# Turning the rows of a second RMSNorm by VectorE block transposes and a round trip through DRAM, instead of by TensorE

## The chip, the cores and the metric

One core of a Trainium2 chip runs the whole kernel in one launch. The metric is the device time of the execution in microseconds (us); lower is better. Engines are named as in the profile: PE is TensorE, PEld its weight loads, DVE is VectorE, ACT is ScalarE, POOL is GpSimd, SP is SyncE, which here only issues DMAs. L970 is line 970 of the kernel before.

## The reference

A single decoder layer with 1024 tokens (and 16 meta tokens), width 1024, feed-forward width 4096, all in fp32. Cut to what matters here:

```python
mix = jnp.concatenate([attn, rec], axis=-1) @ w_out[l]
h = h + rmsnorm(mix, g_post_mix[l])
u = rmsnorm(h, g_pre_ffn[l])                       # the second norm
f = jnp.square(jax.nn.relu(u @ w_ff1[l])) @ w_ff2[l]
h = h + rmsnorm(f, g_post_ffn[l])
```

`u` is computed with a token on each partition, since the norm sums over the width. The product with `w_ff1` contracts over the width, so `u` is needed with the width on the partitions: it has to be transposed.

## The kernel before

Matrix products are done in three matmuls each, on operands split into a high and a low part (`split`, L94: ACT casts the high part, DVE subtracts it from the source for the low part; `mm3`, L123).

The output projection works on eight tiles of 128 tokens (the loop at L1112). For tile t, `out_mm` puts 48 matmuls of 512 columns into two PSUM banks (for tiles 0 to 3 all but 12 of these are done ahead). `out_norm` (L937) then does the following, for each tile:

- SP loads the tile's rows of x into a slot of the ring "d" (four slots) (L939).
- ACT squares both halves out of PSUM and sums them (L944); POOL raises the mean to the power -0.5 (L176).
- DVE scales both halves by that and the gain (L950) and adds the row of x (L953); SP stores the result to the output (L954).
- ACT squares the sum (L956), POOL makes its root (L170, L176), and DVE multiplies by it (L958) into the slot of "d".

`u2_tiles` (L961) turns such a tile: eight 128x128 transposes on PE (L970) into two PSUM banks, each evicted with the gain of the width on its partitions, the first four chunks by ACT (L981), the other four by DVE, two chunks at once (L975). The eight calls stand by hand between the output matmuls of tiles 4 to 7 and behind them (L1115, L1118, L1147). The results, `u2f[half][i]`, are eight tiles of [128, 2, 512] in the ring "c": two chunks of the width by the 512 tokens of one half.

What follows is a feed-forward layer with seven products in place of eight (Strassen's scheme). `operand` (L998) splits the first half's tiles: `b11` after tile 5, `b21` after tile 6. `p1` and `p2` (L1102, L1107) are the first products, of the first half alone. `t_sums` (L1138) forms sums of both halves (L996) and splits them, first for tiles 4 to 6 (three quarters of the columns), later for tile 7. `prep_a` (L1019) loads a pair of weight blocks into the rings "raw" and "d" or "a", sums them on DVE and splits them; `early` (L1045) loads weights ahead. `t_rest` (L1160) makes the later sums.

The order on each engine is set by the program's order as priority, with a planner's estimate of when things are ready; a few orders are written by hand (`behind`). DMAs on SP's queue are issued in order, so a DMA that waits holds up those behind it. Slots of a ring are handed out in turn: whoever takes a slot waits until its last reader is done. "raw" has two slots, "d" four, "ws" five.

Of the kernel before, what the change touches and what calls it, by code (L numbers as in the profile page):

```python
# [9 lines left out]
F32 = mybir.dt.float32  # L10
# [6 lines left out]
P = 128  # L17
D = 1024
# [19 lines left out]
def hybrid_layer(  # L38
# [311 lines left out]
    def transposed(b, xn, after=None):  # L350
        t0, n = ALL[b]
        for kc in range(KC):
            flip[0] += 1
            pt = bank(("pt", "o", "s")[flip[0] % 3])
            o = 0
            for s, m in xn:
                ins = nc.tensor.transpose(
                    pt[:, o : o + m], s[:m, kc * P : (kc + 1) * P], ident[:m, :m]
                )
                if after:  # L360
                    behind(after, ins.ins)
                o += m
            if b == 0:
                load(1, P, ins.ins.name)
            uh, ul = u[kc]
            if b == 0 and kc in (0, 1):
                key_casts.pop(0)()
            high = split_scaled(
                uh[:, t0 : t0 + n], ul[:, t0 : t0 + n], pt[:, :n],
                g_mix_col[:, kc : kc + 1],  # L370
            )
            if b == 0:
                chained(0, high[0])
                chained(1, high[1])

    def fetch(cols, tag="raw", pieces=1):
        raw = slot(tag, [P, KC, P])
# [539 lines left out]
    t4_dram = dpool.tile([P, 2, 4, 512], F32, name="t4_dram")  # L917

    u2f = [[None] * 4 for _ in range(2)]

    def out_mm(t, po, kcs):
        half, o = t // 4, (t % 4) * P
# [8 lines left out]
                )  # L931

    def out_banks(t):
        tag = ("pt", "o", "acc", "s", "pt", "acc", "s", "pt")[t]
        return [bank(tag), bank(tag)]

    def out_norm(t, po):  # L937
        xr = slot("d", [P, D])
        nc.sync.dma_start(xr, x[t * P : (t + 1) * P, :])  # L939
        h = slot("raw", [P, D])  # L940
        ssq = [small.tile([P, 1], F32, name=f"sq{n}", tag=f"sq{n}") for n in range(2)]
        for n in range(2):
            c = slice(512 * n, 512 * n + 512)
            nc.scalar.activation(  # L944
                h[:, c], po[n], AF.Square, scale=RMS_SC, accum_out=ssq[n]
            )
        rs = rstd_of(ssq)
        for n in range(2):
            c = slice(512 * n, 512 * n + 512)
            nc.vector.scalar_tensor_tensor(  # L950
                h[:, c], po[n], rs, gmix_b[:, c], op0=ALU.mult, op1=ALU.mult
            )
        nc.vector.tensor_tensor(h, h, xr, op=ALU.add)  # L953
        nc.sync.dma_start(out[t * P : (t + 1) * P, :], h)  # L954
        ssq2 = small.tile([P, 1], F32, name="ssq", tag="ssq")
        nc.scalar.activation(xr, h, AF.Square, scale=RMS_SC, accum_out=ssq2)  # L956
        rs2 = rstd_of([ssq2])
        nc.vector.tensor_scalar(xr, h, rs2, None, op0=ALU.mult)  # L958
        return xr

    def u2_tiles(t, xn):  # L961
        half = t // 4
        if u2f[half][0] is None:
            u2f[half] = [slot("c", [P, 2, 512]) for _ in range(4)]
        o = (t % 4) * P
        for k4 in range(0, KC, 4):
            pt = bank("o", (P, 4, P))
            for i in range(4):
                kc = k4 + i
                nc.tensor.transpose(pt[:, i, :], xn[:, kc * P : (kc + 1) * P], ident)  # L970
            for i in range(0, 4, 2):
                kc = k4 + i
                dst = u2f[half][kc // 2]
                if k4:
                    nc.vector.tensor_tensor(  # L975
                        dst[:, :, o : o + P], pt[:, i : i + 2, :],
                        g_ffn_col[:, kc : kc + 2].to_broadcast([P, 2, P]), op=ALU.mult,
                    )
                    continue
                for n in range(2):  # L980
                    nc.scalar.activation(  # L981
                        dst[:, n, o : o + P], pt[:, i + n, :], AF.Copy,
                        scale=g_ffn_col[:, kc + n : kc + n + 1],
                    )

# [9 lines left out]
    def combine(dst, x0, x1, op):  # L995
        return nc.vector.tensor_tensor(dst, x0, x1, op=op).ins  # L996
# [115 lines left out]
    for t in range(8):  # L1112
        po = pos[t] if t < 4 else out_banks(t)
        out_mm(t, po, range(6 if t < 4 else 0, KC))
        for t_ in {4: (0,), 5: (2,), 6: (4,), 7: (5,)}.get(t, ()):  # L1115
            u2_tiles(t_, xns[t_])
        xns[t] = out_norm(t, po)
        for t_ in {4: (1,), 5: (3,), 7: (6,)}.get(t, ()):  # L1118
            u2_tiles(t_, xns[t_])
        if t == 4:  # L1120
            a11_early.update(early(0, 0, pair("a", ESH)))
        if t == 5:
            b11 = operand(u2f[0][0:2])
# [7 lines left out]
        p1(p, a11_early[p])  # L1131
    for p in range(2):
        p2(p, a12_early[p])
    t3 = [slot("a", [P, 2, 512]) for _ in range(2)]
    t2 = [slot("a", [P, 2, 512]) for _ in range(2)]
    ot2 = [pair("b", [P, 2, 512]) for _ in range(2)]

    def t_sums(c):  # L1138
        for i in range(2):
            combine(t3[i][:, :, c], u2f[1][2 + i][:, :, c], u2f[1][i][:, :, c], ALU.subtract)  # L1140
            combine(t2[i][:, :, c], t3[i][:, :, c], u2f[0][i][:, :, c], ALU.add)
            hi, lo = ot2[i]
            split(hi[:, :, c], lo[:, :, c], t2[i][:, :, c])

    t_sums(slice(0, 3 * P))
    wa[0] = prep_a(0)
    u2_tiles(7, xns[7])  # L1147
    t_sums(slice(3 * P, 4 * P))
    urgent = mark[0]
    for p in range(2, 4):  # L1150
        p1(p, a11_early[p])
# [1 line left out]
    p2(2, a12_early[2])  # L1153
    ot3 = [pair("b", [P, 2, 512]) for _ in range(2)]
    for i in range(2):
        behind(urgent, split(*ot3[i], t3[i]))
    wa[1] = prep_a(1, urgent)


    def t_rest(k):  # L1160
        i = k % 2
        if k < 2:
            behind(mark[0], combine(u2f[1][i], u2f[1][i], u2f[0][i], ALU.subtract))
        elif k < 4:
            behind(mark[0], combine(t2[i], u2f[0][2 + i], t2[i], ALU.subtract))
        else:
            hl = pair("a", [P, 2, 512])
            late = mark[0]
            behind(late, split(*hl, t2[i]))
# [339 lines left out]
```

## Time and profile before

| | |
|---|---|
| median of 3 runs | 955.24 us (955.24 to 955.97) |
| span of the profiled execution, first to last instruction | 955.3 us |
| mean granted TensorE clock | 0.998 |
| the part that the change touches | about 261 to 352 us of the span |
| DMA traffic over the span | 130.21 MB, mean 136 GB/s |

The profile is one execution, taken by the hardware profiler. The span agrees with the runs to 0.1 us. Busy times of PE overlap, since matmuls are pipelined: a matmul of 512 columns is shown as 0.39 us long, but the next starts 0.23 us later. So lengths of PE's work are read from start to start. A timeline row is: start, length, engine, line, operation, out<-in with shapes, and in brackets how long the engine had been idle and what ended that. A row of groups is: line, engine, operation, shapes, count | busy us, mean ns | idle time before.

### The profile page before, as it was taken

How to read it: one execution, taken by the hardware profiler on the slowest of the kernel's cores; microseconds unless marked ns; L12 is line 12 of the kernel's file. 1: busy time of each engine (PE TensorE's matmuls, PEld its weight loads, DVE VectorE, ACT ScalarE, POOL GpSimd, SP SyncE). 2: the span in 40 equal slices, each digit the busy share in tenths (PEclk: the TensorE clock that was granted, in tenths of full speed). 3: DMA queues.
4: the chain of work that ended last, by engine and by line, in shares of the span. 5: the costliest groups of instructions: out<-in, count | busy, mean ns of one | idle time of the engine just before them, and what ended most of it. 6: DMA issues, size and time to landing. Idle time of an engine off the chain costs nothing.

```text
span 955.3 us, 12432 instructions
## 1 busy us (share of the span) xinstructions
PE 943.8 (99%) x4728; PEld 789.7 (83%) x4728; DVE 655.7 (69%) x845; ACT 505.9 (53%) x854; POOL 129.1 (14%) x189
## 2 busy tenths in 40 slices
PE   9999999999999999999999999999999999999996
PEld 8999999877888878888888888888887788888885
DVE  6567987788856787665644465476667576779893
ACT  7537766568645554444655575654433343446441
POOL 4102563520021100010000000001121100001201
PEclk9999999999999999999999999999999999999999
DMA  8221010204226368674422364334777765647934
GB/s 271 56 67 23 24 45 24 67 23 131 83 109 185 133 220 264 198 253 144 155 89 88 111 203 127 104 113 114 175 180 186 185 199 177 192 139 196 246 65 89
DMA packets 88199, 130.21 MB, mean 136 GB/s; under 512 B 13702, under 2 KB 52630, under 8 KB 88140
## 3 DMA queue, kind: packets, MB, share of 16 engines
q1 hardware_dynamic: 78972, 104.44, 34.0%
q0 software_dynamic: 8880, 24.19, 12.2%
q8 instruction: 37, 0.61, 0.3%
q10 hardware_dynamic: 288, 0.79, 0.2%
q14 instruction: 22, 0.18, 0.1%
HBM read 109.93 MB, written 18.87 MB: 135 GB/s over the span
## 4 chain that ended last, share of the span: by engine, by line
PE 88%; DVE 5%; ACT 3%; DMA 2%; POOL 1%; issue 1%; SPq 0%; DVEq 0%; ACTq 0%; POOLq 0%
PE ps_acc L130 10%; PE ps_acc L131 10%; PE ps_acc L125 10%; PE ps_s L131 6%; PE ps_s L130 6%; PE ps_s L125 6%; PE ps_pt L130 6%; PE ps_pt L131 6%; PE ps_pt L125 6%; PE ps_o L130 5%; PE ps_o L131 5%; PE ps_o L125 5%; ACT c L82 1%; PE ps_o L691 1%; PE ps_acc L282 1%
## 5 line engine op out<-in xcount | busy, mean ns | idle before, releaser
L99 DVE TENSOR_TENSOR ws<-raw,ws 128x1024 fp32r<-128x1024 f32 (+1 forms) x69 | 82.6, 1197 | 76.1 <-ACT ws L96 24.3
L96 ACT CAST ws<-raw 128x1024 fp32r<-128x1024 f32 (+1 forms) x68 | 69.7, 1026 | 87.9 <-PE ps_o L130 23.9
L96 ACT CAST ws<-e 128x1024 fp32r<-128x1024 f32 x41 | 43.0, 1049 | 82.8 <-PE ps_o L130 35.3
L125 PE MATMUL ps_acc<-a,ws 128*128 128x256 f32 (+2 forms) x256 | 85.8, 335 | 0.0
L130 PE MATMUL ps_acc<-a,ws 128*128 128x256 f32 (+2 forms) x256 | 85.5, 334 | 0.0
L131 PE MATMUL ps_acc<-a,ws 128*128 128x256 f32 (+2 forms) x256 | 85.0, 333 | 0.0
L99 DVE TENSOR_TENSOR b<-b,b 128x1024 fp32r<-128x1024 f32 (+2 forms) x50 | 58.9, 1177 | 24.8 <-PE ps_o L130 19.1
L96 ACT CAST b<-b 128x1024 fp32r<-128x1024 f32 (+2 forms) x49 | 49.9, 1019 | 46.4 <-DVE b L996 41.0
L99 DVE TENSOR_TENSOR ws<-e,ws 128x1024 fp32r<-128x1024 f32 x41 | 50.1, 1223 | 32.4 <-ACT ws L96 18.9
L680 POOL TENSOR_SCALAR_AFFINE_SELECT c<-c 128x512 fp32r<-128x512 f32 x64 | 53.6, 858 | 67.6 <-ACT c L96 59.3
L125 PEld LDWEIGHTS ps_acc<-a,ws 128*128 128x128 f32 x256 | 48.3, 189 | 4.7 <-issue 0.2
L131 PEld LDWEIGHTS ps_acc<-a,ws 128*128 128x128 f32 x256 | 48.3, 189 | 4.5
L130 PEld LDWEIGHTS ps_acc<-a,ws 128*128 128x128 f32 x256 | 48.2, 188 | 4.4 <-issue 0.4
L125 PE MATMUL ps_acc<-ws,b 128*128 128x512 f32 (+1 forms) x120 | 46.3, 387 | 1.1 <-ACT ws L96 1.1
L130 PE MATMUL ps_acc<-ws,b 128*128 128x512 f32 (+1 forms) x120 | 46.3, 386 | 0.5 <-DVE ws L99 0.4
L131 PE MATMUL ps_acc<-ws,b 128*128 128x512 f32 (+1 forms) x120 | 46.1, 385 | 0.0
L125 PE MATMUL ps_pt<-ws,b 128*128 128x512 f32 x112 | 44.4, 396 | 0.0
L130 PE MATMUL ps_pt<-ws,b 128*128 128x512 f32 x112 | 44.1, 394 | 0.0
L131 PE MATMUL ps_pt<-ws,b 128*128 128x512 f32 x112 | 44.0, 393 | 0.0
L125 PE MATMUL ps_s<-ws,b 128*128 128x512 f32 x110 | 43.4, 395 | 0.0
L131 PE MATMUL ps_s<-ws,b 128*128 128x512 f32 x110 | 43.3, 394 | 0.0
L130 PE MATMUL ps_s<-ws,b 128*128 128x512 f32 x110 | 43.3, 393 | 0.0
(416 smaller groups left out, 2662.0 us busy)
## 6 DMA issues: line engine op xcount, KB each, us to landing
raw<-in_w_ff_dram SPq DMA_DIRECT2D x61, 512.0 KB, 4.1
e<-in_w_ff_dram SPq DMA_DIRECT2D x45, 512.0 KB, 4.0
a<-in_w_ff_dram SPq DMA_DIRECT2D x12, 512.0 KB, 6.6
s_dram<-a POOLq DMA_DIRECT2D x12, 512.0 KB, 3.7
c<-in_x_dram SPq DMA_DIRECT2D x8, 512.0 KB, 4.0
raw<-in_w_in_dram SPq DMA_DIRECT2D x8, 512.0 KB, 3.7
d<-in_x_dram SPq DMA_DIRECT2D x8, 512.0 KB, 3.3
out_dram<-raw SPq DMA_DIRECT2D x8, 512.0 KB
```

What stands on the lines that cost most here:

```text
L82: ins = nc.scalar.activation(*args, **kwargs).ins
L96: nc.scalar.copy(hi, src)
L99: low = nc.vector.tensor_tensor(lo, src, f32(hi), op=ALU.subtract).ins
L125: ins = nc.tensor.matmul(dst, lh, rh, start=start, stop=False, skip_group_check=True).ins
L130: nc.tensor.matmul(dst, lh, rl, start=False, stop=False, skip_group_check=True)
L131: last_mm[0] = nc.tensor.matmul(dst, ll, rh, start=False, stop=stop, skip_group_check=True).ins.name
L282: last_mm[0] = nc.tensor.matmul(acc[:, :n], w[k // 2][:, kc, :], u[kc][k % 2][:, t0 : t0 + n], start=k == 0 and kc == 0, stop=k == last an ...
L680: nc.gpsimd.affine_select(out=p_[:, :, s], in_=f32(p_[:, :, 0]), pattern=[[0, 4], [g, P]], compare_op=op, fill=0.0, base=0, channel_multip ...
L691: nc.tensor.matmul(po[:, oc : oc + n], v, p_[:, pc : pc + n], start=first and k == 0, stop=last and k == 1, skip_group_check=True,)
```

## The change

Tiles 0 to 6 (`LAST_BY_DMA = 6`) are no longer turned by PE. Instead `out_norm` multiplies the tile by the root and by the gain at once, with the gain broadcast over all partitions (`gpre_b`, a new slot of "ws", loaded once by an ACT DMA). Then `blocks` lets DVE transpose blocks of 32x32 into a second slot of "d" (`y`): it reads each run of 32 elements with a step of four, so that partition p of the result collects what the write then puts in order. One DMA writes the 512 KB to a DRAM scratch with rows of 4 KB. `u2_read`, called one tile later, fetches it by four DMAs of 128 KB, each with runs of 64 floats (256 bytes), straight into the four tiles `u2f[half][i]`. All five transfers are on SP's queue. Tile 7 still goes over PE.

For this the layout of `u2f`, `t2` and `t3` changes from [128, 2, 512] to [128, 16, 2, 32], groups of 32 tokens outermost; `split` writes back into [128, 2, 512] through a rearranged view (`rows`). The evictions of tile 7 are single chunks on both engines. Tile 7's PSUM banks are those of the ring "o" instead of "pt".

```diff
+    def blocks(y, src, dram):
+        nc.vector.transpose(
+            y.rearrange("p (b k t) -> p b k t", b=4, k=KC),
+            src.rearrange("p (k d b) -> p b k d", k=KC, b=4),
+        )
+        nc.sync.dma_start(dram.rearrange("a (d b) r -> (a d) (b r)", b=4), y)
+
+    def unblock(dst, dram, i, n):
+        w = 2 * P // n
+        nc.sync.dma_start(
+            dst.rearrange("p a k t -> p a (k t)"),
+            dram[:, :, w * i : w * i + w].rearrange("a p r -> p a r"),
+        )
...
+    LAST_BY_DMA = 6
+    u2_dram = dpool.tile([LAST_BY_DMA + 1, 4, P, 2 * P], F32, name="u2_dram")
+    gpre_b = slot("ws", [P, D])
+    nc.scalar.dma_start(gpre_b, g_pre_ffn[0].partition_broadcast(P))
...
-        tag = ("pt", "o", "acc", "s", "pt", "acc", "s", "pt")[t]
+        tag = ("pt", "o", "acc", "s", "pt", "acc", "s", "o")[t]
...
-        nc.vector.tensor_scalar(xr, h, rs2, None, op0=ALU.mult)
-        return xr
+        if t > LAST_BY_DMA:
+            nc.vector.tensor_scalar(xr, h, rs2, None, op0=ALU.mult)
+            return xr
+        nc.vector.scalar_tensor_tensor(
+            xr, h, rs2, gpre_b, op0=ALU.mult, op1=ALU.mult
+        )
+        blocks(slot("d", [P, D]), xr, u2_dram[t])
...
+    def u2_read(t):
+        g = slice(4 * (t % 4), 4 * (t % 4) + 4)
+        for i, dst in enumerate(u2_half(t // 4)):
+            unblock(dst[:, g], u2_dram[t], i, 4)
...
+                    d_ = dst[:, g, n]
+                    s_ = pt[:, i + n, :].rearrange("p (a t) -> p a t", a=4)
+                    col = g_ffn_col[:, kc + n : kc + n + 1]
+                    if k4:
+                        nc.vector.tensor_scalar(d_, s_, col, None, op0=ALU.mult)
+                    else:
+                        nc.scalar.activation(d_, s_, AF.Copy, scale=col)
...
+    def rows(tile_, c=slice(0, 16)):
+        return tile_.rearrange("p k (g t) -> p g k t", t=32)[:, c]
...
-            split(hi, lo, t_)
+            split(rows(hi), rows(lo), t_)
...
-        for t_ in {4: (0,), 5: (2,), 6: (4,), 7: (5,)}.get(t, ()):
-            u2_tiles(t_, xns[t_])
         xns[t] = out_norm(t, po)
-        for t_ in {4: (1,), 5: (3,), 7: (6,)}.get(t, ()):
-            u2_tiles(t_, xns[t_])
+        if t:
+            u2_read(t - 1)
```

More of the change, by code (lines that the diff above doesn't have):

```diff
@@ L972, in u2_tiles @@
                 kc = k4 + i
[L973 to L979, printed above, removed]
[L980 to L984 removed]
+                dst = u2_half(t // 4)[kc // 2]
+                for n in range(2):
+                    d_ = dst[:, g, n]
[5 more added lines that the diff above has]
+                        nc.scalar.activation(d_, s_, AF.Copy, scale=col)
     w1v = w_ff1.rearrange("(b k p) c -> b p k c", b=2, p=P)
@@ L1133, in hybrid_layer @@
         p2(p, a12_early[p])
-    t3 = [slot("a", [P, 2, 512]) for _ in range(2)]
-    t2 = [slot("a", [P, 2, 512]) for _ in range(2)]
+    t3 = [slot("a", [P, 16, 2, 32]) for _ in range(2)]
+    t2 = [slot("a", [P, 16, 2, 32]) for _ in range(2)]
     ot2 = [pair("b", [P, 2, 512]) for _ in range(2)]
@@ L1139, in t_sums @@
         for i in range(2):
-            combine(t3[i][:, :, c], u2f[1][2 + i][:, :, c], u2f[1][i][:, :, c], ALU.subtract)
-            combine(t2[i][:, :, c], t3[i][:, :, c], u2f[0][i][:, :, c], ALU.add)
+            combine(t3[i][:, c], u2f[1][2 + i][:, c], u2f[1][i][:, c], ALU.subtract)
+            combine(t2[i][:, c], t3[i][:, c], u2f[0][i][:, c], ALU.add)
             hi, lo = ot2[i]
-            split(hi[:, :, c], lo[:, :, c], t2[i][:, :, c])
-    t_sums(slice(0, 3 * P))
+            split(rows(hi, c), rows(lo, c), t2[i][:, c])
+    t_sums(slice(0, 12))
     wa[0] = prep_a(0)
     u2_tiles(7, xns[7])
-    t_sums(slice(3 * P, 4 * P))
+    t_sums(slice(12, 16))
     urgent = mark[0]
@@ L1155, in hybrid_layer @@
     for i in range(2):
-        behind(urgent, split(*ot3[i], t3[i]))
+        behind(urgent, split(*map(rows, ot3[i]), t3[i]))
     wa[1] = prep_a(1, urgent)
@@ L1168, in t_rest @@
             late = mark[0]
-            behind(late, split(*hl, t2[i]))
+            behind(late, split(*map(rows, hl), t2[i]))
             for n in range(2):
```

9 lines of the change are left out of this document (5 added, 4 removed).

## The prediction

> **What bounds the kernel now.** I read the page first, then the chain that ended last, then the windows and the timelines of TensorE (PE) and VectorE (DVE) around the second norm.
>
> ```profile
> span 955.3 us, 12432 instructions
> PE 943.8 (99%) x4728; PEld 789.7 (83%) x4728; DVE 655.7 (69%) x845; ACT 505.9 (53%) x854; POOL 129.1 (14%) x189
> PE 88%; DVE 5%; ACT 3%; DMA 2%; POOL 1%; issue 1%; SPq 0%; DVEq 0%; ACTq 0%; POOLq 0%
> ```
>
> PE is busy for 99% of the span, and 88% of the chain is PE. So time taken out of PE's queue is worth its full length, unless another engine is close behind it. The windows show where that is so:
>
> ```profile
> 261.00:282.00 21.00, 21.00 (x93) 17.02 (x92) 11.13 (x17) 9.32 (x24) 5.40 (x10) 1.00 0.26 101
> 320.00:335.00 15.00, 15.00 (x78) 12.50 (x77) 12.56 (x21) 8.85 (x23) 2.40 (x4) 1.00 0.55 176
> 335.00:352.00 17.00, 16.94 (x74) 13.34 (x73) 16.20 (x27) 11.83 (x18) 0.56 (x2) 1.00 0.58 189
> ```
>
> After window and length come PE, PEld, DVE, ACT and POOL busy, then the granted clock, the DMA share and GB/s. Until 320 us DVE has slack; from 335 to 352 it works 16.20 of 17.00 us. The chain runs through exactly that stretch:
>
> ```profile
> 319.70 0.87 PE ps_o L970 x8
> 323.39 0.59 ACT d L1105
> 324.03 1.16 ACT d L956 x2
> 325.58 0.99 POOL rs L176
> 326.59 0.26 DVE d L958
> ...
> 350.49 0.61 DVE e L99
> 351.15 0.50 PE ps_acc L131
> ```
>
> The chain leaves PE at 323.4, passes through the last norm (L956, L176, L958 of tile 7), then stays on DVE (with a weight load in between) and gives back to PE at 351.15. There PE is only just not waiting. So whatever PE gains ahead of that point counts only as far as DVE's work moves forward too.
>
> **What the change takes from PE.** It removes seven of the eight groups of eight transposes at L970.
>
> ```profile
> 281.73 0.39 PE L131 MATMUL ps_pt<-a,b 128*128 128x512 f32 x1
> 281.96 1.03 PE L970 MATMUL ps_o<-ident,d 128*128 128x128 f32 x8
> 282.75 0.48 PE L125 MATMUL ps_acc<-ws,b 128*128 128x512 f32 x1
> 283.07 0.40 PE L130 MATMUL ps_acc<-ws,b 128*128 128x512 f32 x1
> ```
>
> Matmuls start every 0.23 us. Without the group the two after it would start at 281.96 and 282.19; the second starts at 283.07, so a group costs 0.88 us of PE. Seven cost **6.2 us**, the most that the change can bring by PE. Five groups stand ahead of the end of tile 7's output matmuls (319.5 us), so that end moves forward by 5 x 0.88 = **4.4 us**. The other two lie between it and 351.
>
> **What it takes from and gives to DVE.** Rows of the groups by form, and one tile's turn in DVE's timeline:
>
> ```profile
> L958 DVE TENSOR_SCALAR d<-raw,rs 128x1024 f32<-128x1024 f32 x8 | 6.0, 754 | 12.8 <-POOL rs L176 12.8
> L975 DVE TENSOR_TENSOR c<-ps_o,gcol 128x256 f32<-128x256 f32 x16 | 6.0, 415 | 0.0
> L953 DVE TENSOR_TENSOR raw<-raw,d 128x1024 f32<-128x1024 f32 x8 | 9.8, 1224 | 0.2
> L1343 DVE SCALAR_TENSOR_TENSOR a<-b,rs,ws 128x1024 f32<-128x1024 f32 x4 | 5.1, 1279 | 0.0
> ...
> L851 DVE TENSOR_TENSOR_SCAN c<-b,c 128x1040 f32<-128x1040 f32 x2 | 4.6, 2314 | 0.0
> ...
> 264.39 1.41 DVE L950 SCALAR_TENSOR_TENSOR raw<-ps_pt,rs,e 128x512 f32<-128x512 f32 x2 [0.75 <-POOL rs L176]
> 275.74 1.41 DVE L950 SCALAR_TENSOR_TENSOR raw<-ps_acc,rs,e 128x512 f32<-128x512 f32 x2
> 280.58 0.75 DVE L958 TENSOR_SCALAR d<-raw,rs 128x1024 f32<-128x1024 f32 x1 [2.10 <-POOL rs L176]
> 281.40 1.41 DVE L950 SCALAR_TENSOR_TENSOR raw<-ps_s,rs,e 128x512 f32<-128x512 f32 x2
> 321.28 1.41 DVE L950 SCALAR_TENSOR_TENSOR raw<-ps_pt,rs,e 128x512 f32<-128x512 f32 x2
> ```
>
> Per tile two evictions of 415 ns go, 0.75 us as a pair in the timeline. The scaling by the row's root grows from a tensor_scalar to a scalar_tensor_tensor with the broadcast gain: 1.28 - 0.75 = +0.53 us. New is the block transpose of 128x1024. The trace has no transpose on DVE and no read with a step of four elements. It can't cost less than the cheapest pass over 128x1024, 0.75 us; the dearest pass over as many elements is the scan, 2.31 us. I take **1.22 us**, the row of the plain two-operand pass at L953, since a transpose too has to move each element once, and keep 0.75 and 2.31 for the range.
>
> In the stretch where eight tiles follow each other, DVE runs one tile's turn after the other: L950, L953, a wait for ACT and POOL, L958, next tile. From 275.74 to 281.40 that is 5.66 us. With the change a turn is 5.66 + 0.53 + 1.22 = 7.41 us if the transpose stands ahead of the next tile's L950. Tile 7's L950 then comes no sooner than 264.39 + 7 x 7.41 = 316.3 us. PE would let it come at 321.28 - 4.4 = 316.9. The two nearly meet: DVE's turns become almost the bound, with 0.6 us to spare. The weight and operand splits that also lie here must fit into the waits of some 2.1 us per turn (the row at 280.58). In sum that fits, but not each one; I charge **0.6 us**.
>
> Within the chain's stretch after L958 of tile 7, tile 6's pair of evictions (0.75) goes; tile 7's second four chunks are now evicted by four instructions instead of two, for which no row exists: I charge 0.4 for them (two more starts of short instructions; bounds 0 and 0.8). Net -0.35. The sums and splits at L996 and L99 see other strides of whole 32-element runs; I cost them at nothing, since the rows at L996 that already read halves of a row run at the speed of the others:
>
> ```profile
> L996 DVE TENSOR_TENSOR raw<-raw 128x512 f32<-128x512 f32 x16 | 10.9, 688 | 0.3
> L99 DVE TENSOR_TENSOR b<-b,b 128x512 fp32r<-128x512 f32 x4 | 2.7, 679 | 0.0
> ```
>
> ACT loses 28 evictions and gains one DMA issue for the gain; ACT was ahead of nothing here. The changed bank for tile 7 (tile 1's) is long free.
>
> **The transfers.** Each tile now writes 512 KB and reads it back in four parts with runs of 256 bytes.
>
> ```profile
> 270.38 0.60 ACT L944 ACTIVATE raw<-ps_acc 128x512 f32<-128x512 f32 x1 [2.13 <-DMA out_dram<-raw]
> ...
> 267.08 11.68 SPq L954 DMA_DIRECT2D out_dram<-raw  x3
> ...
> L208 SPq DMA_DIRECT2D raw<-in_w_in_dram x13: 368/368/817, 23.0 to 170.8; - x13
> ...
> DMA to landing us min/median/max: 3.0/3.6/3.7
> ...
> s_dram<-a POOLq DMA_DIRECT2D x12, 512.0 KB, 3.7
> ...
> a<-in_w_ff_dram SPq DMA_DIRECT2D x12, 512.0 KB, 6.6
> ```
>
> A write of 512 KB lands after 3.3 (issued 267.08, its waiter starts at 270.38) to 3.7 us, loads in pieces of 64 columns (L208, the same 256-byte runs) after 3.0 to 3.7, and an issue holds SP 0.37 us. For tiles 0 to 5 there is room: their operands are split after 305. Tile 6 decides. Its turn ends at 316.3 at the earliest (where tile 7's L950 starts); the write lands by 320.4; its reads stand behind tile 7's store, which waits for L953 of tile 7 (316.9 + 1.41 + 1.14 = 319.5). So four issues run from 320.4 to 321.9 and the last lands at about 325.2. What reads tile 6 first, the sums of three tiles, starts now at 328.52 and should move to 328.52 - 4.4 - 0.75 = 323.4:
>
> ```profile
> 328.52 0.95 DVE L996 TENSOR_TENSOR a<-c,c 128x768 f32<-128x768 f32 x1
> ```
>
> So the sums come up to 1.8 us late; DVE has weight sums to do first (L996 on raw, 0.6 each), so I charge **0.7 us**. While SP waits for the write, loads of the next weights stand behind it, for at most those 1 to 2 us; the row copies of x need their slot of d two tiles later and come in time at 7.4 us per turn.
>
> **Sum.** DVE's stretch moves forward by 4.4 + 0.35 - 0.6 - 0.7 = 3.45 us, PE by 6.2. PE then waits for the difference, 2.75 us, and the end moves by 3.45. The profiled execution spans 955.3 us and the median of the runs is 955.24, so I subtract from the latter: 955.24 - 3.45 = **951.8 us**.
>
> **Rivals.**
> - *PE's whole gain.* After 352 DVE has idle time again, and if the order of DVE's work changes so that less stands ahead of the split at 350.49, all 6.2 us arrive: 949.0. For it: only a few waits of DVE are in the stretch. Against it: DVE is 95% busy there.
> - *Late transfers.* Under load, loads take 6.6 us (row above) instead of 3.6. Then tile 6 arrives 3 us later, the sums wait for it with nothing else ahead of them on DVE, and of the 3.45 us only 0.45 is left: **954.8**, no change. (Were the write as slow, 2.9 us more: 957.7.) For it: the x rows, output rows and weights run in the same time, and seven tiles move 1 MB more each. Against it: the DMA share was 0.26 from 261 to 282 and 0.55 from 320 to 335.
> - *The strided transpose takes double.* At 2.31 us, the scan's row, a turn is 8.50 us and tile 7's L950 comes at 264.39 + 7 x 8.50 = 323.9, 2.6 us later than before. With -0.35, the 0.6 for splits that don't fit and 0.7 for tile 6, the end moves back by 3.5: **958.8 us**, slower. It decides from about 1.8 us per transpose: there a turn is 8.0 us, tile 7's L950 comes at 320.4, 0.9 sooner than before, and 0.35 + 0.9 pays just for the 0.6 + 0.7. What speaks for it is that each 32-element run is read with a step of 16 bytes, which nothing in the trace does; against it, that DVE's plain passes run alike whatever their runs. [...]
> - *The change costs more on the queues.* SP carries five more issues a tile, each behind a wait; if weight loads fall behind, the products after 341 us wait for them: 960 and more.
>
> **How the numbers follow.** The forecast has 0.47, PE's whole gain 0.08, late transfers 0.13, the double transpose 0.24, the queues 0.08. A measurement of this kernel can tell about 0.2% (1.9 us) from no change. The first two are faster: 0.55; the third is the same: 0.13; the last two slower: 0.32. The forecast alone spans 949.5 to 953.3. The range that holds 8 in 10 reaches from PE's whole gain, 949.0, to just over the double transpose, 959.5.
>
> **What would show it.** In the profile after: seven groups at L970 gone and out_mm of tiles 5 to 7 closed up; the transposes' mean, 1.2 or 2.3 us, read off their row; the start of tile 7's L950 on DVE, 316 to 317 us if right, 324 if the strided read doubles; the first sum of tiles 4 to 6, waiting for a DMA or not; and PE's idle time between 335 and 352, 2 to 3 us if DVE bounds it. The forecast is wrong if the transposes lie above 1.8 us, or if the order of DVE's work around the last two tiles is another than now.

## The result, and the profile after

The changed kernel takes **969.78 us**, the median of five runs (968.66 to 974.73); beside it the kernel before took 955.24 us (955.02 to 955.97). The ratio is 1.0159, with a 95% interval of 1.0137 to 1.0181: 14.5 us slower, where 3.4 us faster was forecast and 959.5 was the end of the range. The profiled execution is the longest of the five, 974.73 us with a span of 973.0; of its excess 3.5 us arise at 737 to 775 us, behind late weight loads, and belong to this execution. The rest is the stage of the second norm.

The busy times on the page after:

```profile
PE 942.9 (97%) x4672; PEld 787.3 (81%) x4672; DVE 668.2 (69%) x840; ACT 498.5 (51%) x826; POOL 128.6 (13%) x189
```

PE has lost 56 matmuls but hardly any busy time, DVE has gained 12.5 us, and on the same page the DMA packets under 512 bytes have doubled (28614 after 13702). In the chain that ended last PE has gone from 88% to 82%.

The windows of after (window, length, PE, PEld, DVE, ACT, POOL busy, granted clock, DMA share, GB/s), the three that were shown of before and the next one:

```profile
261.00:282.00 21.00, 21.00 (x92) 17.09 (x91) 13.05 (x15) 7.59 (x20) 3.17 (x7) 1.00 0.46 148
320.00:335.00 15.00, 12.37 (x54) 9.67 (x52) 12.06 (x14) 5.29 (x10) 1.88 (x4) 1.00 0.83 244
335.00:352.00 17.00, 3.61 (x11) 2.40 (x11) 13.41 (x22) 8.57 (x17) 1.77 (x3) 0.50 0.89 278
352.00:370.00 18.00, 17.60 (x70) 14.27 (x71) 13.26 (x21) 8.10 (x12) 1.08 (x2) 0.91 0.50 153
```

Up to 282 us DVE has 1.9 us more to do, and PE shows nothing yet. From 335 to 352 PE works 3.61 of 17 us instead of 16.94, at half the clock. Behind that, the same instruction runs 14.0 us later than before from 355 us on, and this offset stays until about 690. So the whole loss, but for the 3.5 us of this execution, arises between 261 and 355. DVE's timeline there (start, length, engine, line, operation; L969, L972 and L978 are the former L950, L953 and L958):

```profile
270.76 1.40 DVE L969 SCALAR_TENSOR_TENSOR raw<-ps_o,rs,e 128x512 f32<-128x512 f32 x2
272.08 1.99 DVE L378 STREAM_TRANSPOSE d<-d 128x1024 f32<-128x1024 f32 x1
273.99 1.18 DVE L972 TENSOR_TENSOR raw<-raw,d 128x1024 f32<-128x1024 f32 x1
278.54 1.41 DVE L969 SCALAR_TENSOR_TENSOR raw<-ps_acc,rs,e 128x512 f32<-128x512 f32 x2
283.09 1.23 DVE L972 TENSOR_TENSOR raw<-raw,d 128x1024 f32<-128x1024 f32 x1 [1.25 <-DMA d<-in_x_dram]
287.69 1.40 DVE L969 SCALAR_TENSOR_TENSOR raw<-ps_s,rs,e 128x512 f32<-128x512 f32 x2
336.60 1.22 DVE L972 TENSOR_TENSOR raw<-raw,d 128x1024 f32<-128x1024 f32 x1 [2.59 <-DMA d<-in_x_dram]
340.38 0.75 DVE L978 TENSOR_SCALAR d<-raw,rs 128x1024 f32<-128x1024 f32 x1 [0.46 <-POOL rs L176]
```

The transpose takes 2.0 us and stands, with the next tile's L969 already done, ahead of the add L972. From the second tile's start to the third's it is 7.78 us; from there to the fourth's 9.15, since the add waits for the row of x. Such waits are 7.6 us in all. The last scaling starts at 340.38 instead of 326.59, 13.8 us late, and the loss is 14.0. SP's queue shows why the rows are late (L382 is the write to scratch, L386 the four reads, L958 the row of x):

```profile
274.09 0.33 SPq L382 DMA_DIRECT2D u_dram<-d  x1
275.20 0.34 SPq L973 DMA_DIRECT2D out_dram<-raw  x1
276.73 2.02 SPq L386 DMA_DIRECT2D c<-u_dram  x4
278.81 0.50 SPq L958 DMA_DIRECT2D d<-in_x_dram  x1
```

The slot for the next row of x is free when the transpose ends, at 274.07. But the row is issued behind the four reads, at 278.81, and lands at 283. The first read waits for the write to land, from 274.09 to 276.73, and issuing the four then takes 2.02 us. Weights stand in the same queue: the first ones loaded ahead were issued at 287.93 before, and now at 296.63 and 299.21. ACT waits for them, with tile 5's squares queued behind its cast. ACT's timeline, before and then after:

```profile
291.97 1.05 ACT L96 CAST a<-raw 128x1024 fp32r<-128x1024 f32 x1 [1.82 <-DMA raw<-in_w_ff_dram]
```

```profile
303.67 1.05 ACT L96 CAST a<-raw 128x1024 fp32r<-128x1024 f32 x1 [9.34 <-DMA raw<-in_w_ff_dram]
```

PE's timeline of after shows what became of its 6.2 us:

```profile
341.19 1.97 PE L1001 MATMUL ps_o<-ident,d 128*128 128x128 f32 x8 [8.82 <-DVE d L978]
349.46 0.79 PE L125 MATMUL ps_pt<-b,a 128*128 128x512 f32 x1 [6.30 <-ACT a L96]
353.42 0.63 PE L130 MATMUL ps_pt<-b,a 128*128 128x512 f32 x1
353.85 0.63 PE L131 MATMUL ps_pt<-b,a 128*128 128x512 f32 x1
```

PE has run out of work at 332.4, waits 8.82 us for the last tile, then 6.30 for a cast. After the first wait the eight transposes take 1.97 us instead of 1.03, and until 355.3 matmuls start 0.43 us apart instead of 0.23.

### The profile page after: what moved, and what is told of

Same layout as the page of the kernel before. It is cut to its first block, busy times and chain, and to the rows that moved or that the text cites. A ratio compares the mean times of both kernels' runs of the same rounds, so it can differ in the third digit from the quotient of the medians.

```text
span 973.0 us, 12341 instructions
## 1 busy us (share of the span) xinstructions
PE 942.9 (97%) x4672; PEld 787.3 (81%) x4672; DVE 668.2 (69%) x840; ACT 498.5 (51%) x826; POOL 128.6 (13%) x189
## 2 busy tenths in 40 slices
DMA packets 104134, 138.06 MB, mean 142 GB/s; under 512 B 28614, under 2 KB 67542, under 8 KB 104076
## 4 chain that ended last, share of the span: by engine, by line
PE 82%; DVE 6%; DMA 4%; ACT 3%; issue 2%; POOL 1%; SPq 1%; DVEq 0%; ACTq 0%; POOLq 0%
PE ps_acc L130 10%; PE ps_acc L131 10%; PE ps_acc L125 10%; PE ps_s L130 6%; PE ps_s L131 6%; PE ps_s L125 6%; PE ps_pt L131 5%; PE ps_pt L130 5%; PE ps_pt L125 5%; PE ps_o L130 5%; PE ps_o L125 5%; PE ps_o L131 5%; DMA d<-in_x_dram 2%; DMA raw<-in_w_ff_dram 1%; ACT c L82 1%
## 5 line engine op out<-in xcount | busy, mean ns | idle before, releaser
L125 PE MATMUL ps_pt<-ws,b 128*128 128x512 f32 x110 | 43.5, 395 | 0.0
L130 PE MATMUL ps_pt<-ws,b 128*128 128x512 f32 x110 | 43.3, 394 | 0.0
L131 PE MATMUL ps_pt<-ws,b 128*128 128x512 f32 x110 | 43.3, 393 | 0.0
```

The costliest lines, as they stand in the source:

```text
L125: ins = nc.tensor.matmul(dst, lh, rh, start=start, stop=False, skip_group_check=True).ins
L130: nc.tensor.matmul(dst, lh, rl, start=False, stop=False, skip_group_check=True)
L131: last_mm[0] = nc.tensor.matmul(dst, ll, rh, start=False, stop=stop, skip_group_check=True).ins.name
```

## The experiments

The theory at this point: the norms' turns on DVE got longer (transpose, then x rows held up on SP), PE only waits for them, and the halved clock adds to it. The rivals: the new layout costs something; the transfers themselves do; PE's time matters all the same. Each run is compared with runs of the kernel before on the same chip. A tile starts with its L950. "Offset" is how much later than before one and the same eviction runs (at 414.5 us in the profile of before), in the profiled execution.

| run | tile 4 starts | tile 7 starts | last scaling | offset | median | above before |
|---|---|---|---|---|---|---|
| before | 287.07 | 321.28 | 326.59 | 0 | 955.24 | 0 |
| the change | 296.52 | 331.44 | 340.38 | 14.0 | 969.78 | 14.5 |
| layout alone | 287.19 | 321.79 | 326.67 | 0.2 | 956.79 | 1.3 |
| plain read | 295.49 | 329.88 | 338.77 | 13.7 | 969.80 | 14.3 |
| x first | 293.68 | 328.80 | 333.68 | 8.1 | 964.39 | 8.9 |
| no transpose | 288.78 | 324.34 | 330.75 | 3.9 | 960.39 | 4.9 |
| x first, plain read | 291.08 | 326.65 | 331.54 | 4.9 | 961.82 | 5.6 |
| x first, late weights | 293.62 | 326.53 | 331.89 | 8.2 | 964.36 | 8.2 |
| x first, four tiles | 293.69 | 327.73 | 334.94 | 9.8 | 966.06 | 9.9 |
| x first, late weights, plain | 290.99 | 321.59 | 327.74 | 4.4 | 962.51 | 6.3 |
| x first, PE busy (misplaced) | 293.32 | 328.45 | 333.34 | 16.4 | 974.41 | 18.4 |
| transpose in the wait | 288.45 | 324.26 | 329.82 | 4.6 | 961.13 | 5.1 |
| four tiles, in the wait | 287.99 | 321.25 | 327.09 | 2.3 | 959.64 | 3.6 |
| PE still busy | 295.30 | 329.42 | 337.29 | 11.9 | 968.64 | 12.6 |
| x first, PE busy in place | 293.54 | 328.67 | 333.55 | 6.1 | 963.67 | 7.3 |
| four transposes alone | 291.83 | 323.90 | 329.03 | 4.5 | 960.32 | 3.9 |
| the same, in the wait | 288.63 | 322.17 | 327.06 | 0.6 | 956.32 | -0.1 |

In most rows the offset follows the last scaling: where that is late by so much, the offset is the same within some 2 us. The two runs with late weights stand out: their offsets are 2.9 and 3.2 us larger than the last scaling is late. The misplaced matmuls are a case of their own.

**Layout alone.** All eight tiles over PE at the places of before, with the new layout and evictions.

```diff
-    LAST_BY_DMA = 6
+    LAST_BY_DMA = -1
...
+        for t_ in {4: (0,), 5: (2,), 6: (4,), 7: (5,)}.get(t, ()):
+            u2_tiles(t_, xns[t_])
         xns[t] = out_norm(t, po)
-        if t:
-            u2_read(t - 1)
+        for t_ in {4: (1,), 5: (3,), 7: (6,)}.get(t, ()):
+            u2_tiles(t_, xns[t_])
```

> All eight tiles go over PE as before; only the layout of u2f, t2, t3 (groups of 32 tokens outermost), the split through a rearranged view, and the single-chunk evictions are those of the change. Theory 1 (the loss is in the new path of the rows): 955 us, within 1 us of before. Rival (strided splits and sums cost DVE and ACT time in the stretch that DVE bounds): 957 us and more, with longer means of the sums and splits.

956.79 us, ratio 1.0008 (0.9997 to 1.0018). The layout costs nothing that can be told from zero; that rival is out.

**Plain read.** The transpose reads runs of 32 elements that lie side by side, so that the products take rows in another order of the width.

```diff
-            src.rearrange("p (k d b) -> p b k d", k=KC, b=4),
+            src.rearrange("p (k b d) -> p b k d", k=KC, b=4),
```

> The block transposes read each run of 32 elements without a step (the rows then come out in another order of the width, so the product is of permuted rows); all transfers and orders stay. Theory V (the step of four makes a transpose 2.0 us instead of 1.2, and these 0.8 us in each of seven turns in a row are the loss): transposes of about 1.2 us and some 960 to 963 us. Rival Q (rows of x come late, since SP holds their load behind the reads): the transposes may get shorter, but the adds go on waiting for the rows of x, and the time stays over 966 us. Rival: the step costs nothing, the transposes stay at 2.0 us, and so does the time.

The transposes' rows of groups, of after and then of this run (count | busy us, mean ns | idle before):

```profile
L378 DVE STREAM_TRANSPOSE d<-d 128x1024 f32<-128x1024 f32 x7 | 14.1, 2011 | 0.0
```

```profile
L378 DVE STREAM_TRANSPOSE d<-d 128x1024 f32<-128x1024 f32 x7 | 8.7, 1239 | 0.0
```

The step of four costs 0.77 us per transpose. Yet the time stays: 969.80, ratio 1.0143 (1.0117 to 1.0170). The waits for rows of x rise from 7.6 to 10.6 us:

```profile
DVE raw L972 <- DMA d<-in_x_dram: 10.6, 5, 3.5
```

So in the change as it is, the rows of x bound the turn, and a faster transpose only waits longer.

**x first.** The row of x of the next tile is issued ahead of the reads of the last one, which are bound behind it.

```diff
         xns[t] = out_norm(t, po)
+        if t < 7:
+            x_rows(t + 1)
         if t:
-            u2_read(t - 1)
+            u2_read(t - 1, x_ins.get(t + 1))
```

> The load of the next tile's rows of x is issued on SP ahead of the four reads of the tile before, by an order written by hand; all else as in the change. Theory Q: DVE no longer waits for the rows of x (7.6 us in four waits after the change), PE waits that much less, 959 to 963 us. Rival V: DVE's turns are as long as before by their own work, the rows are early and DVE waits for something else, 967 us and more.

964.39 us, ratio 1.0086 (1.0065 to 1.0108): some 5.6 us of the loss go with this order alone. The waits for x are gone, and the turns of tiles 1 to 3 are an even 7.8 us. 8.9 us of loss are left.

**x first, plain read.** Both edits together.

> The rows of x ahead of the reads (as in e3) and the transposes without the step of four (as in e2; the rows come out in another order). Theory now: with the rows of x early, the length of a transpose counts, 0.76 us in each of the first turns; tile 7's last scaling comes 2 to 4 us sooner than e3's 333.7, and the time is 960 to 962 us. Rival (the weight loads on SP and the ACT casts that wait for them set tiles 5 to 7, whatever DVE does): within 1.5 us of e3's 964.4.

961.82 us, ratio 1.0057 (1.0040 to 1.0073). Now the faster transpose counts: 3.3 us less by the medians (the intervals just overlap), 3.2 less by the offset. This run has what the prediction took for granted, a transpose of 1.24 us and x rows in time, and is still 5.6 us slower than before. Its DVE timeline from tile 5 on shows where (L976 is after's L969, L987 the scaling with the gain, after's L980):

```profile
302.80 1.41 DVE L976 SCALAR_TENSOR_TENSOR raw<-ps_acc,rs,e 128x512 f32<-128x512 f32 x2 [0.67 <-POOL rs L176]
306.39 2.35 DVE L99 TENSOR_TENSOR b<-c,b 128x1024 fp32r<-128x1024 f32 x2
309.50 1.29 DVE L987 SCALAR_TENSOR_TENSOR d<-raw,rs,ws 128x1024 f32<-128x1024 f32 x1 [0.76 <-POOL rs L176]
311.84 1.22 DVE L99 TENSOR_TENSOR ws<-raw,ws 128x1024 fp32r<-128x1024 f32 x1
312.98 1.24 DVE L378 STREAM_TRANSPOSE d<-d 128x1024 f32<-128x1024 f32 x1
314.92 1.41 DVE L976 SCALAR_TENSOR_TENSOR raw<-ps_s,rs,e 128x512 f32<-128x512 f32 x2 [0.66 <-POOL rs L176]
319.81 1.29 DVE L987 SCALAR_TENSOR_TENSOR d<-raw,rs,ws 128x1024 f32<-128x1024 f32 x1 [2.22 <-POOL rs L176]
321.01 1.22 DVE L99 TENSOR_TENSOR e<-raw,b 128x1024 fp32r<-128x1024 f32 x1
322.15 1.24 DVE L378 STREAM_TRANSPOSE d<-d 128x1024 f32<-128x1024 f32 x1
326.05 0.69 DVE L1150 TENSOR_TENSOR d<-ps_pt,d 128x512 f32<-128x512 f32 x1 [2.02 <-PE ps_pt L131]
326.65 1.40 DVE L976 SCALAR_TENSOR_TENSOR raw<-ps_o,rs,e 128x512 f32<-128x512 f32 x2
```

The turns of tiles 4, 5 and 6 take 11.7, 12.1 and 11.7 us, not 7.4: the splits of weights and operands stand between the steps of a norm, on DVE and in the same way on ACT, and they are not hidden in its waits. The last turn shows it piece by piece. PE is through with tile 7's output matmuls at 314.7. ACT's timeline for tile 7's squares, before (the second half) and then in this run (the first):

```profile
319.74 0.60 ACT L944 ACTIVATE raw<-ps_pt 128x512 f32<-128x512 f32 x1 [2.35 <-PE ps_pt L131]
```

```profile
321.18 0.60 ACT L970 ACTIVATE raw<-ps_o 128x512 f32<-128x512 f32 x1 [1.42 <-DVE d L987]
```

Before, the squares wait for PE; here they wait until tile 6 is scaled, 6.5 us after PE was through. Squares and weight blocks share the two slots of the ring "raw". In this run one slot holds tile 6 until its scaling, and the other a weight block, which is only split at 321.01. No run gave the ring a third slot, so this reason is read from the trace and the program, not tested. Then a split and a transpose stand on DVE ahead of tile 7's factor, and an eviction of a first product (L1150), which waits 2.02 us for PE, stands ahead of its L976. Before, that eviction came behind tile 7's norm, at 330.60.

**No transpose.** Rows are written to scratch unturned, so that of the change only the transfers and their queue remain.

> The block transposes are left out: the scaled rows are written to the scratch as they are (so the products take rows that are not turned), and the ring d holds no second slot per tile. Writes, reads and their places on SP stay. Theory V+Q (both the 2.0 us on DVE and the ring that makes x wait for the transpose): 950 to 953 us, PE's whole gain of some 5 us. Rival (the transfers themselves, or the reads' places on SP, cost the time): over 960 us.

960.39 us, ratio 1.0044 (1.0028 to 1.0061). The theory's 950 to 953 was missed. Tile 4 starts 1.7 us later than before, since with the longer scaling a turn takes 6.0 us instead of 5.7, and tile 5 starts at 304.74 instead of 296.54. Its ACT timeline:

```profile
301.28 1.05 ACT L96 CAST a<-raw 128x1024 fp32r<-128x1024 f32 x1 [8.61 <-DMA raw<-in_w_ff_dram]
```

The weights are issued at 293.97, behind reads and rows on SP, and tile 5's squares stand behind their cast. So with PE's 6.2 us spared and no transpose, the transfers still make it slower, through the queue.

**x first, late weights; and the same with the plain read.** The weights loaded ahead (`early`) are called one tile later, so that no cast waits in front of the squares.

> The rows of x ahead of the reads (as in e3), and the early weight blocks are asked for one tile later, so that ACT's casts of them, which wait for the load, stand behind the squares of the next tile instead of ahead of them. Transposes as in the change. Theory (ACT stands in front of a weight cast for its load while tile 5's squares wait behind it): tile 5's turn begins some 5 us sooner, the time is 957 to 961 us. Rival (the length of DVE's turns bounds): no sooner than 963 us, or slower, since the weights come later still for the first products.

> All three: rows of x ahead of the reads, weight blocks asked for a tile later, transposes without the step (rows in another order). If the three delays add up, this is the fastest of the seven-tile versions, 953 to 958 us. If it is no faster than e6, the length of the transposes is hidden once the queues are in order.

964.36 us, ratio 1.0091 (1.0072 to 1.0111), and 962.51, ratio 1.0065 (1.0043 to 1.0086). The last scaling comes 1.8 and 3.8 us sooner than with the weights in their old place, in the second run only 1.15 us later than before, and nothing is gained, where 957 to 961 and 953 to 958 were expected: the products that use these weights come late instead. In the second run PE idles in waits of 2.6, 2.0 and 1.4 us. Between these two runs the shorter transpose is worth 1.9 us by the medians, with intervals that overlap, and 3.8 by the offset.

**x first, four tiles.** Tiles 4 to 7 go over PE again (`LAST_BY_DMA = 3`, with x first).

> Only tiles 0 to 3 go by DVE and DRAM, tiles 4 to 7 over PE at their places of before; the rows of x are ahead of the reads. PE saves four groups, 3.5 us. Theory (the cost is the delay of the last tiles' rows, by turns that grow and queues that fill): the last tiles catch up, 952 to 956 us. Rival (the first four tiles alone fill the queues enough to hold up the weights): over 958 us.

966.06 us, ratio 1.0101 (1.0084 to 1.0118), no better than with seven and far from the expected 952 to 956: the turns of tiles 1 to 3, where the harm begins, are the same 7.8 us, and tile 5 starts later still (308.67 against 305.52).

**PE still busy.** The change, with PE doing seven groups of eight transposes of the identity at the places of before (`pe_only`, its result unused).

```diff
+        for t_ in {4: (0,), 5: (2,), 6: (4,), 7: (5,)}.get(t, ()):
+            pe_only()
         xns[t] = out_norm(t, po)
+        for t_ in {4: (1,), 5: (3,), 7: (6,)}.get(t, ()):
+            pe_only()
```

> The change, with TensorE still doing seven groups of eight transposes at the places of the kernel before (of the identity matrix, and nobody uses the result): 7 x 0.88 = 6.2 us of PE work given back. Theory (all that TensorE is spared is spent standing still before the last tile's norm, and the clock falls then): 966 to 970, no slower than the change itself (969.78). Rival (the 6.2 us are saved and the loss is larger by them): 975 to 977.

968.64 us, ratio 1.0131 (1.0103 to 1.0159): no slower than the change without that work. Its PE timeline:

```profile
338.19 1.06 PE L1007 MATMUL ps_o<-ident,d 128*128 128x128 f32 x8 [0.35 <-DVE d L978]
```

The wait of 8.82 us for the last tile has shrunk to 0.35, by more than the 6.2 us put back: the last scaling also comes 3.1 us sooner, for which no cause is shown. All that the change spares PE is spent standing still.

**x first, PE busy.** The halved clock was to be taken away by extra matmuls in the hole.

> The kernel with x rows first (964.39), and 38 matmuls of 512 columns whose results nobody uses: 10 behind the products of third 3 of the first half's weights and 28 behind the last tile's transposes. They fill time in which TensorE waits for the last tile's norm and for weight casts, up to about 38 x 0.22 = 8.4 us of PE work. Theory (part of the loss is the clock that halves after TensorE has stood still): the granted clock in 335 to 355 stays near 1.00 (0.60 without them) and the time falls by some 3 us to 960 to 962. Rival (the clock's fall costs nothing because the stretch is set by the casts and the norm): 964 to 966. Second rival (the extra matmuls stand in the way of useful ones): 967 and more.

974.41 us, ratio 1.0192 (1.0160 to 1.0223). The run missed its aim: the extra matmuls ran behind 363 us, where PE has no gap. Their 8.7 us cost 9.4 by the distances to before and 8.3 by the offsets. It shows only that behind this stage PE's time does count in full. The repeat bound 60 transposes of the identity into the hole:

```diff
+    for j in range(60):
+        busy = nc.tensor.transpose(pb[:, j % 4, :], ident, ident).ins
+        behind(u2_end, busy)
+        u2_end = busy.name
...
-    p2(2, a12_early[2])
+    p2(2, a12_early[2], u2_end)
```

> The kernel with x rows first (964.39), with 60 transposes of the identity matrix, whose results nobody uses, bound between the last tile's transposes and the products that wait 7.5 us for weight casts there: at 0.11 us each (a group of eight 0.88) some 6.9 us of work in a hole of 7.5. In the run with 38 extra matmuls these went elsewhere and showed only that 8.7 us of PE work behind 366 us cost 10. Theory (the halved clock costs by itself): the matmuls behind the hole start 0.23 us apart instead of 0.43, and the time falls by 2 to 4 us to 960.5 to 962.5. Rival (the casts and the weights set the stretch, the clock costs nothing): 964 to 966 with the clock at full.

963.67 us, ratio 1.0063 (1.0042 to 1.0085). PE's timeline around the hole and its window from 335 to 355 us, first with x first alone, then with the filling:

```profile
334.49 1.10 PE L1010 MATMUL ps_o<-ident,d 128*128 128x128 f32 x8 [2.58 <-DVE d L985]
343.09 0.79 PE L125 MATMUL ps_acc<-b,e 128*128 128x512 f32 x1 [7.50 <-ACT b L96]
346.95 0.63 PE L130 MATMUL ps_acc<-b,e 128*128 128x512 f32 x1
347.38 0.63 PE L131 MATMUL ps_acc<-b,e 128*128 128x512 f32 x1
335.00:355.00 20.00, 12.10 (x40) 8.70 (x39) 19.97 (x33) 10.83 (x19) 0.65 (x1) 0.66 0.60 179
```

```profile
335.29 6.71 PE L1197 MATMUL ps_pt<-ident 128*128 128x128 f32 x60
342.94 0.50 PE L125 MATMUL ps_acc<-b,e 128*128 128x512 f32 x1 [0.94 <-ACT b L96]
347.40 0.40 PE L130 MATMUL ps_pt<-b,a 128*128 128x512 f32 x1
347.64 0.39 PE L131 MATMUL ps_pt<-b,a 128*128 128x512 f32 x1
335.00:355.00 20.00, 17.82 (x108) 14.79 (x106) 19.34 (x32) 11.01 (x19) 0.65 (x1) 1.00 0.69 202
```

With the hole filled, matmuls start 0.23 us apart from the first, but for waits; without, 0.43 apart for 7.3 us. The granted clock of the window is 1.00 instead of 0.66 (the first run's expectation gives it as 0.60). The offset falls by 2.0 us, the median's distance to before by 1.7, with intervals that overlap. So the clock did what the theory said, and its fall costs about 2 us by the profiles, which the medians alone don't tell from nothing. The median lies between the theory's numbers and the rival's: DVE is busy for 19.97 of these 20 us without the filling and 19.34 with it, and PE still waits for DVE and ACT (0.9 and 0.7 us).

**Transpose in the wait; four tiles of it.** For tiles 0 to 3 the transpose is moved behind the next tile's add, where DVE waits for POOL; its output goes to the ring "c", so "d" again holds four rows of x, and the reads come a tile later. In the second run only tiles 0 to 3 go through scratch.

```diff
         xns[t] = out_norm(t, po)
+        if 0 < t < 5:
+            blocks(slot("c", [P, D]), xrs[t - 1], u2_dram[t - 1], adds[t])
+        for t_ in {2: (0,), 3: (1,), 4: (2,), 5: (3, 4), 6: (5,), 7: (6,)}.get(t, ()):
+            u2_read(t_)
```

> The change, but the block transpose of tiles 0 to 3 runs behind the next tile's add of x rows instead of before it, in the time in which VectorE waits for GpSimd's scaled rows; its output goes to the ring of the scaled rows, so that four rows of x lie in their own ring; the read transfers of tiles 0 to 3 go one tile later. Theory (the loss begins with the transpose in the serial part of the norm's turn and with x rows that come late): turns of tiles 0 to 4 of about 6.2 us in place of 9, the last scaling at 331 to 334 in place of 340.4, time 956 to 961. Rival (the transposes' and transfers' total work sets it, wherever it stands): turns of 7.5 us and more, 964 to 970.

> As the kernel with the transpose in the wait, but only tiles 0 to 3 go by the block transpose and scratch memory; tiles 4 to 7 are transposed by TensorE at the places of the kernel before. Theory: VectorE's part of the last four norms is that of before and TensorE is spared 4 x 0.88 = 3.5 us; the last scaling's start is 328 to 330 (326.6 before), and what TensorE saves is partly idle again: 953 to 958, about the kernel before. Rival (late weights and the transfers cost it as much as with seven tiles): 961 to 966.

961.13 us, ratio 1.0054 (1.0038 to 1.0071), and 959.64, ratio 1.0028 (1.0016 to 1.0040). The first turns are 6.0 us in both, as expected: two thirds of the change's loss go with the transpose's place, the ring and the later reads. The second run came out slower than the expected 953 to 958. With four tiles the last norm stands where it stood before (327.09 against 326.59) and PE was spared 3.5 us, yet nothing is won: up to 356 us the offset is 0.5, not negative, and waits for weight casts at 362 make it 2.3. No version tried beats the kernel before.

**Four transposes alone; the same in the wait.** The kernel of layout alone, plus the block transposes of tiles 0 to 3 with unused results and no transfer, at the change's place and then behind the next add.

```diff
             nc.vector.tensor_scalar(xr, h, rs2, None, op0=ALU.mult)
+            if t < 4:
+                y = slot("c", [P, D])
+                nc.vector.transpose(
+                    y.rearrange("p (b k t) -> p b k t", b=4, k=KC),
+                    xr.rearrange("p (k d b) -> p b k d", k=KC, b=4),
+                )
```

> The kernel of layout alone (956.79: TensorE turns all eight tiles), with the block transposes of tiles 0 to 3 added at the change's place, their results unused, and no transfer. Theory (what stands between scaling and the next add on VectorE lengthens the chain of norms): turns of the first four tiles of 7.7 us instead of 5.7, the last scaling at 329 to 333 instead of 326.6, 959 to 964. Rival (the loss is the transfers' and the queue's; VectorE has room): 956 to 957.5.

> As the kernel with four transposes alone, but each behind the next tile's add, in the wait for GpSimd's factors. Theory: turns of 6.0 to 6.1 us as in the two kernels with the transpose in the wait, the last scaling within 2 us of before, 956.5 to 959. Rival (it is the transposes' total work, not their place): as the kernel with the transposes at the change's place, 959 to 964.

960.32 us, ratio 1.0039 (1.0023 to 1.0056), against 956.32, ratio 0.9996 (0.9983 to 1.0009). DVE's timelines, at the change's place and then in the wait:

```profile
276.99 1.41 DVE L966 SCALAR_TENSOR_TENSOR raw<-ps_acc,rs,e 128x512 f32<-128x512 f32 x2
278.32 1.98 DVE L978 STREAM_TRANSPOSE c<-d 128x1024 f32<-128x1024 f32 x1
284.41 1.41 DVE L966 SCALAR_TENSOR_TENSOR raw<-ps_s,rs,e 128x512 f32<-128x512 f32 x2
```

```profile
276.17 1.41 DVE L968 SCALAR_TENSOR_TENSOR raw<-ps_acc,rs,e 128x512 f32<-128x512 f32 x2
278.76 2.03 DVE L1150 STREAM_TRANSPOSE c<-d 128x1024 f32<-128x1024 f32 x1
281.02 0.75 DVE L977 TENSOR_SCALAR d<-raw,rs 128x1024 f32<-128x1024 f32 x1 [0.19 <-POOL rs L176]
281.84 1.41 DVE L968 SCALAR_TENSOR_TENSOR raw<-ps_s,rs,e 128x512 f32<-128x512 f32 x2
```

The same instruction makes a turn 7.42 us in one place, and 5.67, as long as before, in the other, where it fills the wait of 2.1 us down to 0.19. Where the wait is no longer empty it costs there too: the turn of tile 3, in which the evictions of tile 0 (1.08 us) stand behind the transpose, takes 6.79 us. Over the whole kernel, four transposes cost 3.9 us at the change's place and nothing measurable in the wait. It is the place that costs, not the work.

## Why the prediction was wrong, step by step

The forecast missed by 18.0 us (-3.4 against +14.5). The runs divide this: from the change to x first 5.6, from there to the plain read 3.3, and 9.0 that remain with both premises met (5.6 slower instead of 3.4 faster). The last part is what is left over, and no single run stands for it.

- *PE's part* held: without the groups PE was through with tile 7's output matmuls at 315.5 instead of 319.5 us, 4.0 sooner where 4.4 was forecast.
- *"PE would let it come at 321.28 - 4.4"*, with DVE's turns of 7.41 us as the only other bound, failed, and it is the costliest step: the 9.0 us begin here. In before, tile 7's squares did wait for PE. But with PE out of the way tile 7's L950 did not follow, nor did DVE's bare turns set it. It came at 326.65 in the run with both premises met, 9.8 us behind the forecast's 316.9. Up to tile 4 the bare turns were right, even a little long (291.08, where 264.39 + 4 x 7.41 gives 294.0). The three turns behind that take 35.6 us in place of 22.2. That these turns are longer could be seen in before: there they take 34.2 us (287.07 to 321.28), partly waiting for PE, and not 3 x 5.66. The forecast measured a turn of tiles that have no splits beside them and carried it to tiles that have. I had added up the splits' work and charged 0.6 us; what counted is that each piece stands inside the chain of a norm.
- *The transpose at 1.22 us* was mis-sized: 2.01 with the step of four. Without the step it is 1.24, so the row chosen was right for the plain form. The rival "takes double" had the cause, the step, and the 2.01 us lie above the 1.8 from which it was to decide, but its 958.8 holds only this one cause. The step's own price is 1.9 to 3.3 us by the medians once x rows come in time, and nothing visible before.
- *"The row copies of x ... come in time"* failed: 5.6 us. `y` takes every second slot of "d", so that a row can't be loaded until the tile two before is turned, and then it stands on SP behind four reads that wait for a write. I had looked at the slot and not at the queue in front of the issue.
- *"Loads of the next weights stand behind it, for at most those 1 to 2 us"* failed in size: the first cast waits 9.34 us. By itself that was not shown to cost: with the weights asked for one tile later, the time was the same 964.4.
- *"PE then waits for the difference, 2.75 us"*: from 261 us on, PE needs 106.6 us of busy time until it stands 14.0 us behind, against 108.9 up to the same point before (the windows above; from 282 to 320 PE is fully busy in both). 6.2 us of work are gone, so slow matmuls stretch the rest by 3.8, and it stands idle for the other 16.4: 16.4 + 3.8 - 6.2 = 14.0. That PE came back from its waits of 8.82 and 6.30 us at a granted clock of 0.50 was no term of the sum; filling the hole gives 2 us back by the offset.
- The sign *"if the order of DVE's work around the last two tiles is another than now"* came true: the eviction that stood behind tile 7's norm in before stands ahead of it with both premises met.
- *The layout at nothing* held (ratio 1.0008). The 0.4 us for tile 7's four evictions was an estimate with no row behind it; after shows 1.04 us for the four from start to start (0.26 each), 0.38 more than the pair's 0.66. The transfer's own time at tile 6, 0.7 us, did not come to bear, since everything came later.

What stays open is how the 9.0 us divide between DVE's order, ACT's order and the ring "raw". The two runs with late weights moved the weights' splits a tile on. With the plain read this shortened the three turns from 35.6 to 30.6 us and brought the last scaling to within 1.15 us of before, and the time stayed, with the weights late instead. So an early last norm alone was not enough; no run had both.

## What to carry to other kernels

Time that is taken from the busiest engine is worth only as much as the chain that feeds it can move forward: put the spared work back as dummies, and if the time stays the same (968.64 us against 969.78 here), the engine was only waiting. An added instruction on a side engine costs nearly its full length inside a serial chain (1.75 of 1.98 us here) and nothing in one of the chain's waits, as long as it fits there (turns of 7.42 against 5.67 us), so place it before adding up busy time. A turn read off one stretch holds for another only if the same work stands beside it: compare it with that other stretch in the trace of before. On a queue that issues in order, as SP's did here (the row of x whose slot was free at 274.07 us was issued at 278.81, behind four reads), list what stands behind each DMA that has to wait for another DMA.

## What the runs showed of the hardware

A transpose of 128x1024 fp32 in 32x32 blocks on DVE takes 1.24 us with contiguous runs, about as much as a plain two-operand pass (1.22), and 2.01 us when it reads with a step of 16 bytes. The step is a factor of 1.6 here.

After 7.5 and 8.8 us of standing still, PE's matmuls of 512 columns started 0.43 us apart instead of 0.23, for 7.3 us (x first) and up to 355.3 us (the change, with further waits of 6.30 and 1.30 us between). In the change the granted clock was 1.00 up to 334.8 us, 2.4 us after PE had run out of work, and 0.50 from 335.0 to 355.2. From 355.4 on it was 1.00 again, 3.0 us after the last of the waits had ended at 352.40. Shorter waits went both ways. In x first a single wait of 2.58 us left the eight transposes behind it at 1.10 us. In x first with late weights and the plain read a wait of 2.63 us stretched them to 1.64, and matmuls followed 0.43 us apart, for some 3 us in all:

```profile
328.55 1.64 PE L1010 MATMUL ps_o<-ident,d 128*128 128x128 f32 x8 [2.63 <-DVE d L985]
```

Two waits of 2.24 and 0.79 us within 4 us (four transposes alone) were followed by 3 us at 0.43, too. The runs show how these waits came out, not what decides it, and the slow stretches differ too: 3 us here, 7.3 in x first.
